# Upward stage of a feed-forward block: pinned squares, later use of mixed blocks, evacuation in parts

## The chip, the cores and the metric

The kernel runs on one core of one Trainium2 chip. Its time is the device time of one launch in microseconds (us), the median of several runs. The core has five engines with a queue each, which run their instructions in order: PE (TensorE, matmul), DVE (VectorE), ACT (ScalarE), POOL (GpSimd) and SP (SyncE), which here issues nearly all DMAs. PEld is PE's loading of weights.

## The reference

One block of a diffusion transformer on 2048 tokens of width 1024. A mixer comes first (gated linear attention and retention, both directions), then a convolutional feed-forward part, then a norm. The change concerns the weights of both, and above all the upward half of the feed-forward part:

```python
def _conv_ffn(h, w_up_l, conv_w_l, conv_b_l, w_down_l):
    gate, up = jnp.split(h @ w_up_l, 2, axis=-1)
    L = gate.shape[1]
    pad = CONV_W // 2
    gp = jnp.pad(gate, ((0, 0), (pad, pad), (0, 0)))
    gate = sum(gp[:, j:j + L] * conv_w_l[j] for j in range(CONV_W)) + conv_b_l
    return (jax.nn.silu(gate) * up) @ w_down_l
```

D_FF is 2816, CONV_W 3, and all inputs are float32.

## The kernel before

**Products.** Every big product is made of half-precision pairs (a high part and the rest), three matmuls for one (`mm3`, lines 84 to 86), and of 2x2 blocks with seven block products instead of eight (a Strassen-like scheme, Winograd's form). The left factor needs seven mixed blocks: four raw ones a11, a12, a21, a22 and three sums of them; two of the products, 0 and 1, use raw blocks alone. `left_blocks` yields them step by step; `emit` makes the high part on ACT and the rest on DVE, `add` makes the sums on POOL, in place.

**The upward stage** (`ffn_up`) goes over 11 pairs of column blocks j (columns j and j + 11 of 22). For each j it runs four *units*: `ty` 0 (gate) and 1 (up), each for the token halves t 0 and 1. A unit is seven passes of 12 matmuls of 128x512, which `unit` takes in the order 0, 1, 5, 6, 4, 3, 2; after passes 1, 4, 3 and 2 `evac` takes a result away. For the gate (`gate_evac`) this is the convolution: a centre tap on ACT, the two side taps on DVE, the edges to the neighbouring blocks, and a Silu when a half is whole. For up (`up_evac`) it is a product with the gate.

**Background work.** Between the passes `work(n)` draws n steps from a list of generators, `self.bg`, first come first served:

- `up_weights(j, ty)` loads two raw tiles `wur` (SP), squares them on ACT (line 1474, the sum of squares by row comes with it), sums the squares over rows by 16 matmuls with a column of ones (`col`, line 1476) and over everything by two more (`allsum`, line 107), derives a scale on DVE, and makes the seven blocks `w7`.
- `down_blocks(j)` loads two rows of the down weights, `wdb`, squares them on ACT (line 1513), forms four differences in place on POOL (line 1516), and stores them to `wdd`.
- `act_pairs(j, t, act)` makes the seven mixed blocks of the activations as pairs `st` and stores them to `actd` (seven stores for each half).

`wur` and `wdb` share the tag "wr", which has two buffers. So the up half's blocks must be done before the down rows can be loaded, and the down rows' differences must be stored before the gate weights of j + 1 can be loaded.

**Order.** The program's order is a priority only. A scheduler with a timing model sets the order of instructions on each engine when the kernel is built, and waits are put in after that; so code that moves in one place can turn the order elsewhere. `keep_in_program_order`, used by the change, holds an instruction in the program's order on its engine.

Of the kernel before, what the change touches and what calls it, by code (L numbers as in the profile page):

```python
# [18 lines left out]
P = 128  # L19
SEQ = 2048  # L20
D = 1024
# [21 lines left out]
RING = 10  # L43
SEQUENCE = 0, 1, 5, 6, 4, 3, 2
# [6 lines left out]
class Kern:  # L51
# [427 lines left out]
    def left_blocks(self, a, emit, add):  # L479

        a11, a12, a21, a22 = a
        emit(0, a11)
        yield
        emit(1, a12)
        yield
        emit(3, a22)
        add(a22, a21, a22, ALU.add)  # L487
        yield
        emit(4, a22)
        add(a21, a11, a21, ALU.subtract)  # L490
        yield
        emit(6, a21)
        add(a11, a22, a11, ALU.subtract)
        yield
        emit(5, a11)
        add(a12, a12, a11, ALU.subtract)
        yield
        emit(2, a12)
        yield
# [136 lines left out]
    def pair_blocks(self, raws, W, s, neg):  # L636

        nc = self.nc

        def emit(m, v):  # L640
            sc = neg if m == 3 else s
            nc.scalar.activation(W[m][:, 0], v, AF.Copy, scale=sc)  # L642
            nc.vector.scalar_tensor_tensor(W[m][:, 1], v, sc, W[m][:, 0], ALU.mult, ALU.subtract)  # L643
        blocks = [r[:, 4 * c:4 * c + 4] for r in raws for c in range(2)]
        yield from self.left_blocks(blocks, emit, nc.gpsimd.tensor_tensor)

    def scales(self, ssq, dqx, tag, bank="tu"):

        nc, kp = self.nc, self.kp
        s, i = self.pow2(self.wp, self.allsum(ssq, bank), 1, "w")  # L650
# [9 lines left out]
    def head_weights(self, h):  # L660
# [11 lines left out]
        for nm, tag, cols in want:  # L672
# [7 lines left out]
            def start(nm=nm, tag=tag, raws=raws, st=st):  # L680
# [7 lines left out]
                s, neg, dq = self.scales(ssq, self.dqx[:, 0:1] if h else None, "dq" + nm)  # L688
# [10 lines left out]
            def more(st=st):  # L699
                next(st["steps"], None)  # L700
                next(st["steps"], None)
# [757 lines left out]
    def up_weights(self, j, ty):  # L1459
# [10 lines left out]
        ssq = kp.tile([P, 2], F32, tag="ssqw2", bufs=2, name="ssqw")  # L1470
        col = self.ps("sc", [P, 2], "col")
        for i in range(2):
            sq = W[5 + i].rearrange("p a k n -> p (a k n)").bitcast(BF16)
            nc.scalar.activation(sq, raw[i].rearrange("p k n -> p (k n)"), AF.Square, scale=4.0, accum_out=ssq[:, i:i + 1])
            for k in range(KT):
                nc.tensor.matmul(col[:, i:i + 1], sq[:, k * P:(k + 1) * P], self.onesb, start=k == 0 and i == 0,
                                 stop=k == KT - 1 and i == 1, skip_group_check=True)
        yield
        s, neg, dq = self.scales(ssq, self.dqx[:, 1:2], ("dqz", "dqvg")[ty], "sc")
# [23 lines left out]
    def down_blocks(self, j):  # L1503
# [7 lines left out]
        for i, r in enumerate(rows):  # L1511
            junk = self.slot_tile([P, D], F16, "vg", "st")
            nc.scalar.activation(junk, r, AF.Square, scale=self.ias[:, j:j + 1], accum_out=self.wq[:, 2 * j + i:2 * j + i + 1])
# [22 lines left out]
    def gate_evac(self, j, t, act, ends):  # L1536

        nc = self.nc
        tap = self.W[j, 0][1]
        stt = nc.vector.scalar_tensor_tensor  # L1540

        def evac(f, half, c, s):
# [6 lines left out]
            nc.scalar.activation(a[:, o:o + G], c, AF.Identity, bias=self.cw[:, fi:fi + 1], scale=tp(1))  # L1549
# [3 lines left out]
            nc.scalar.copy(edge[:, n], view(c, 0, [[G - 1, 2]]))  # L1553
            stt(a[:, o + 1:o + G], c[:, :G - 1], tp(0), a[:, o + 1:o + G], ALU.mult, ALU.add)
            stt(a[:, o:o + G - 1], c[:, 1:], tp(2), a[:, o:o + G - 1], ALU.mult, ALU.add)
            ends[f][n] = True
            col = lambda x, i: act[x // 2][f][:, x % 2 * G + i:x % 2 * G + i + 1]
            for x in (n - 1, n):
                if x in ends[f] and x + 1 in ends[f] and x < 3:
                    stt(col(x, G - 1), edge[:, x + 1, 0:1], tp(2), col(x, G - 1), ALU.mult, ALU.add)  # L1560
                    stt(col(x + 1, 0), edge[:, x, 1:2], tp(0), col(x + 1, 0), ALU.mult, ALU.add)
            if n == 2:
                nc.scalar.activation(act[0][f], act[0][f], AF.Silu)
            if t and 2 in ends[f] and 3 in ends[f]:
                nc.scalar.activation(a, a, AF.Silu)
# [11 lines left out]
    def act_pairs(self, j, t, act):  # L1577
# [4 lines left out]
        def emit(m, v):  # L1582
            p = self.slot_tile([P, 2, G], F16, "vg", "st")
            nc.scalar.activation(p[:, 0], v, AF.Copy, scale=s)  # L1584
            nc.vector.scalar_tensor_tensor(p[:, 1], v, s, p[:, 0], ALU.mult, ALU.subtract)  # L1585
            nc.sync.dma_start(self.actd[m][t][:, j], p)
        blocks = [act[f][:, c * G:c * G + G] for c in range(2) for f in range(2)]
        yield from self.left_blocks(blocks, emit, nc.gpsimd.tensor_tensor)

    def ffn_up(self):  # L1590
        for j in range(NJ):
            self.bg.append(self.up_weights(j, 1))
            act = [[self.slot_tile([P, 2 * G], F32, KEPT[2 * ((2 * j + t) % 3) + f], "act") for f in range(2)] for t in range(2)]
            ends = [{}, {}]
            for ty in range(2):
                for t in range(2):
                    evac = self.gate_evac(j, t, act, ends) if ty == 0 else self.up_evac(j, t, act)
                    for _ in self.ffn_unit(self.W[j, ty][0], self.feats[t], evac, t):
                        self.work(2)
                    if ty == 0 and t == 0:  # L1600
                        self.bg.append(self.down_blocks(j))
                    if ty == 1:
# [214 lines left out]
```

## Time and profile before

| what | value |
| --- | --- |
| runs of the kernel | 2800.43 us median of 3 (2798.17 to 2802.12) |
| the profiled execution | 2800.01 us, span 2797.2 us |
| granted clock of PE, mean | 0.962 |
| mixer and output product | 0 to 1503.84 us |
| upward stage | 1503.84 to 2386.52 us |
| downward stage | 2386.52 to 2797.2 us |

The span goes from the first instruction to the last; the run's time holds a little more around it. In the profile's rows, `L84 PE MATMUL pa<-feat,w` is a matmul issued by line 84 that writes a PSUM tile named pa and reads the tiles feat and w. A wait row names the engine that waited, then whom it waited for.

### The profile page before, as it was taken

To read this page: it belongs to the slowest core of one execution; us is meant where nothing else is said; L and a number is where in the kernel's file an instruction comes from. 1 tells how busy PE (TensorE), PEld (TensorE's weight loads), DVE (VectorE), ACT (ScalarE), POOL (GpSimd) and SP (SyncE) were. 2 spreads that over 40 slices of the span, in tenths; PEclk is the share of its full clock that TensorE was granted. 3 is DMA by queue.
4 is the path that set the end of the run, shared out by engine and by line. 5 is a ranking of instruction groups with operands and counts; after the bars stand their busy time and mean duration, and the time that the engine had idled before them with its cause. 6 is when DMAs were issued, how large, how long until landed. Compare 5 with 4: busy or idle time off the path is not lost.

```text
span 2797.2 us, 56207 instructions
## 1 busy us (share of the span) xinstructions
PE 2575.3 (92%) x22829; PEld 1696.0 (61%) x22829; DVE 1820.0 (65%) x3568; ACT 1335.1 (48%) x2858; POOL 773.9 (28%) x905
## 2 busy tenths in 40 slices
PE   5789998999988988898999999999999999999998
PEld 2678887888888877887444444444444444444443
DVE  4998676776666565456465777677777777532553
ACT  5776456564543433345445555555555554411211
POOL 3642121121222222112334443334333333000111
PEclk7899999999999999998999999999999999999999
DMA  8224332342447675656621322232233323743652
GB/s 289 99 92 145 126 122 92 130 145 88 137 167 235 195 247 178 218 185 185 207 91 46 98 95 93 104 109 95 95 105 102 106 94 138 263 183 141 224 188 102
DMA packets 213523, 402.35 MB, mean 144 GB/s; under 512 B 16271, under 2 KB 98419, under 8 KB 208656
## 3 DMA queue, kind: packets, MB, share of 16 engines
q1 hardware_dynamic: 209856, 390.20, 41.1%
q10 hardware_dynamic: 3104, 8.40, 1.1%
q8 instruction: 178, 2.92, 0.4%
q14 instruction: 81, 0.66, 0.1%
q0 software_dynamic: 304, 0.17, 0.0%
HBM read 298.57 MB, written 91.75 MB: 140 GB/s over the span
## 4 chain that ended last, share of the span: by engine, by line
PE 54%; DVE 21%; DMA 9%; ACT 6%; issue 6%; POOL 4%; ACTq 0%; SPq 0%; DVEq 0%; POOLq 0%
PE pa L84 5%; PE pa L85 5%; PE pa L86 5%; PE pd L85 5%; PE pd L84 5%; PE pd L86 5%; PE pc L84 2%; PE pc L85 2%; PE pc L86 2%; DVE w L643 2%; DMA wur<-in_w_up_dram 2%; PE opp L86 2%; PE opp L85 2%; PE opp L84 2%; DMA wdb<-in_w_down_dram 2%
## 5 line engine op out<-in xcount | busy, mean ns | idle before, releaser
L84 PE MATMUL pa<-feat,w 128*128 128x512 f16 x704 | 267.0, 384 | 10.9 <-ACT ta L543 10.3
L85 PE MATMUL pa<-feat,w 128*128 128x512 f16 x704 | 270.4, 384 | 0.0
L86 PE MATMUL pa<-feat,w 128*128 128x512 f16 x704 | 268.9, 385 | 0.0
L85 PE MATMUL pd<-wd,actl 128*128 128x512 f16 x616 | 233.3, 379 | 0.0
L86 PE MATMUL pd<-wd,actl 128*128 128x512 f16 x616 | 233.3, 379 | 0.0
L84 PE MATMUL pd<-wd,actl 128*128 128x512 f16 x616 | 232.6, 379 | 0.6 <-ACT wd L1627 0.6
L85 PEld LDWEIGHTS <-w 128*128 128x128 f16 x1232 | 121.5, 99 | 157.4 <-issue 21.3
L86 PEld LDWEIGHTS <-w 128*128 128x128 f16 x1232 | 121.5, 99 | 148.6 <-issue 5.8
L84 PEld LDWEIGHTS <-w 128*128 128x128 f16 x1232 | 123.2, 100 | 143.2 <-issue 5.7
L85 PEld LDWEIGHTS <-hx 128*128 128x128 f16 x1824 | 185.9, 102 | 15.9 <-issue 13.4
L84 PEld LDWEIGHTS <-hx 128*128 128x128 f16 x1824 | 186.1, 102 | 2.3
L86 PEld LDWEIGHTS <-hx 128*128 128x128 f16 x1824 | 185.4, 102 | 3.1 <-issue 1.9
L1585 DVE SCALAR_TENSOR_TENSOR st<-act,modT,st 128x512 f16<-128x512 f32 x154 | 146.3, 975 | 55.8 <-ACT st L1584 55.8
L84 PE MATMUL pa<-w_vg,hx 128*128 128x128 f16 x800 | 151.3, 227 | 7.5 <-ACT ct L543 3.9
L85 PE MATMUL pa<-w_vg,hx 128*128 128x128 f16 x800 | 151.1, 227 | 0.0
L86 PE MATMUL pa<-w_vg,hx 128*128 128x128 f16 x800 | 151.1, 227 | 0.0
L1584 ACT ACTIVATE st<-act,modT 128x512 f16<-128x512 f32 x154 | 107.5, 718 | 79.8 <-POOL act L487 19.6
L84 PE MATMUL pc<-feat,w 128*128 128x512 f16 x352 | 135.1, 384 | 2.8 <-ACT tb L543 1.5
L643 DVE SCALAR_TENSOR_TENSOR w<-wur,p2s,w 128x512 f16<-128x512 f32 x132 | 111.1, 859 | 37.2 <-ACT w L642 37.2
L85 PE MATMUL pc<-feat,w 128*128 128x512 f16 x352 | 134.6, 382 | 0.0
L86 PE MATMUL pc<-feat,w 128*128 128x512 f16 x352 | 134.1, 382 | 0.0
L85 PEld LDWEIGHTS <-w_z 128*128 128x128 f16 x1072 | 108.0, 101 | 37.4 <-issue 25.7
(549 smaller groups left out, 7565.3 us busy)
## 6 DMA issues: line engine op xcount, KB each, us to landing
hx<-hxd SPq DMA_DIRECT2D x212, 512.0 KB, 4.8
actd<-st SPq DMA_DIRECT2D x154, 256.0 KB, 2.0
actl<-actd SPq DMA_DIRECT2D x28, 1024.0 KB, 5.1
wur<-in_w_up_dram SPq DMA_DIRECT2D x44, 512.0 KB, 4.0
raw<-in_w_in_dram SPq DMA_DIRECT2D x36, 512.0 KB, 4.5
wm<-in_w_mod_dram SPq DMA_DIRECT2D x64, 256.0 KB, 4.8
hxd<-hx SPq DMA_DIRECT2D x28, 512.0 KB, 3.4
wdb<-in_w_down_dram SPq DMA_DIRECT2D x22, 512.0 KB, 3.6
```

Of the source, the lines that this page charges most:

```text
L84: mm(ps, lhs(0), rhs(0), start=start, stop=False, skip_group_check=True)
L85: mm(ps, lhs(0), rhs(1), start=False, stop=False, skip_group_check=True)
L86: mm(ps, lhs(1), rhs(0), start=False, stop=stop, skip_group_check=True)
L643: nc.vector.scalar_tensor_tensor(W[m][:, 1], v, sc, W[m][:, 0], ALU.mult, ALU.subtract)
L1584: nc.scalar.activation(p[:, 0], v, AF.Copy, scale=s)
L1585: nc.vector.scalar_tensor_tensor(p[:, 1], v, s, p[:, 0], ALU.mult, ALU.subtract)
```

## The change

1. `left_blocks` has separate calls for the high part (`hi`) and the rest (`lo`), a step apart. Block 3 comes first, the three POOL sums follow in the next steps, and the blocks that use them come behind: 3, 0, 1, 4, 6, 5, 2. It yields nine steps instead of seven; the mixer's weights, which use it too, take three steps at a time instead of two.
2. In `up_weights` the two squares are a step each, pinned in the program's order on ACT; an empty step follows; the sums on PE come after it, and the scale a step later. The down rows' squares are pinned too.
3. `gate_evac` no longer issues its parts at once: centre, sides and Silu go into `self.parts`, and `follow` issues one part of each after each pass.
4. `ffn_up` hands out the loads ahead (`ahead`, with idle steps), starts both halves of j + 1 while j runs, waits for what is needed (`until`), and draws 1.7 or 2.3 steps a pass for gate and up, instead of 2.

```diff
-    def left_blocks(self, a, emit, add):
+    def left_blocks(self, a, hi, lo, add):
...
+        hi(3, a22)
+        yield
+        lo(3, a22)
+        hi(0, a11)
         add(a22, a21, a22, ALU.add)
         yield
-        emit(4, a22)
+        lo(0, a11)
+        hi(1, a12)
         add(a21, a11, a21, ALU.subtract)
...
+        for i in range(2):
+            self.tc.keep_in_program_order(nc.scalar.activation(sqs[i], raw[i].rearrange("p k n -> p (k n)"), AF.Square, scale=4.0,
+                                                               accum_out=ssq[:, i:i + 1]))
+            yield
+        yield
         col = self.ps("sc", [P, 2], "col")
...
-        yield
-        s, neg, dq = self.scales(ssq, self.dqx[:, 1:2], ("dqz", "dqvg")[ty], "sc")
+        total = self.allsum(ssq, "sc")
+        yield
+        s, neg, dq = self.scales(total, self.dqx[:, 1:2], ("dqz", "dqvg")[ty])
...
+            self.parts.append([centre, sides, silu])
...
+    def ahead(self, steps, idle=0):
+        next(steps)
+        yield
+        for _ in range(idle):
+            yield
+    def follow(self):
+        for p in self.parts:
+            p.pop(0)()
+        self.parts = [p for p in self.parts if p]
+    def until(self, steps):
+        while steps in self.bg:
+            self.work(1)
...
+    def ffn_pair(self, j, U):
+        act = []
+        ends = [{}, {}]
+        D = self.down_blocks(j)
+        self.bg += [U[j, 1], self.ahead(D, 3)]
+        for ty in range(2):
+            self.until(U.pop((j, ty), None))
+            for t in range(2):
...
+                for _ in self.ffn_unit(self.W[j, ty][0], self.feats[t], evac, t):
+                    self.due += RATE[ty] if j else 2
+                    self.work(int(self.due))
+                    self.due -= int(self.due)
+                    self.follow()
+                if ty == 1:
+                    U[j, "act", t] = self.act_pairs(j, t, act[t])
+                    self.bg.append(U[j, "act", t])
+            if ty == 0:
+                self.bg.append(D)
+                if j + 1 < NJ:
+                    for i, idle in ((0, 4), (1, 0)):
+                        U[j + 1, i] = self.up_weights(j + 1, i)
+                        self.bg.append(self.ahead(U[j + 1, i], idle))
+                        if i == 0:
+                            self.bg.append(U[j + 1, 0])
```

What the scheduler makes of it, at three places of the pair j = 5. First ACT, from the down rows' squares (`st<-wdb`) to the squares of the next gate weights (`w7<-wur`). Before:

```order
L1513 ACTIVATE st_25668,modT_162<-wdb_25651,modT_162 128x1024
L1563 ACTIVATE act_25382<-act_25382 128x1024
L1513 ACTIVATE st_25670,modT_162<-wdb_25653,modT_162 128x1024
L543 COPY ta_25606<-pa_25608 128x512
L543 COPY ta_25753<-pa_25755 128x512
L1549 ACTIVATE act_25385<-ta_25606,cw_161,taps_25159 128x512
L1553 COPY edge_25498<-ta_25606 128x2
L1474 ACTIVATE w7_25778,ssqw_25780<-wur_25769 128x1024
```

After, from the centre tap of the gate's last pass (line 1576) on:

```order
L1576 ACTIVATE act_25533<-pa_25538,cw_161,taps_25227 128x512
L1577 COPY edge_25416<-pa_25538 128x2
L1594 ACTIVATE act_25534<-act_25534 128x1024
L1533 ACTIVATE st_25771,modT_162<-wdb_25730,modT_162 128x1024
L1533 ACTIVATE st_25773,modT_162<-wdb_25732,modT_162 128x1024
L554 COPY ta_25734<-pa_25736 128x512
L1594 ACTIVATE act_25533<-act_25533 128x1024
L554 COPY tb_25735<-pc_25801 128x512
L1488 ACTIVATE w7_25834,ssqw_25836<-wur_25797 128x1024
```

The down squares moved from the middle of the gate's second unit to behind its last pass (`pa_25538`), and the weights' squares from among that unit's evacuation to behind the first copies of the unit after it (`pa_25736`, `pc_25801`).

Second PE, where the first sums of those squares stand. Before, `pa_25755` is the first up unit, in its pass 5:

```order
L84 MATMUL pa_25755<-feat_20720,w7_25507 128x512
L85 LDWEIGHTS w7_25507
L85 MATMUL pa_25755<-feat_20720,w7_25507 128x512
L86 LDWEIGHTS w7_25507
L86 MATMUL pa_25755<-feat_20720,w7_25507 128x512
L1476 LDWEIGHTS w7_25778
L1476 MATMUL col_25781<-onesb_21514,w7_25778 128x1
```

After, `pb_25927` is the second up unit, in its pass 1:

```order
L85 MATMUL pb_25927<-feat_21595,w7_25553 128x512
L86 LDWEIGHTS w7_25553
L86 MATMUL pb_25927<-feat_21595,w7_25553 128x512
L1495 LDWEIGHTS w7_25834
L1495 MATMUL col_25866<-onesb_21514,w7_25834 128x1
```

The sums moved by most of a unit. Counted in these orders, PE has 126 matmuls of passes between the up total (`allsum`) and these sums before, 147 after; and from their own total to the first use of the new gate blocks 102 before, 30 after. For the up half's blocks that is 72 before and 33 after. In the mixer's stage PE's order changes too, in some 240 places from the first projection on, with the same instructions.

Third SP, where the raw up weights of j + 1 are loaded. Before, behind one store of activation pairs:

```order
L1466 DMA wur_25771<-in_w_up_dram 128x8x128
L1586 DMA actd00_93<-st_25938 128x1024
L1466 DMA wur_26151<-in_w_up_dram 128x8x128
L1466 DMA wur_26153<-in_w_up_dram 128x8x128
L1586 DMA actd10_95<-st_25942 128x1024
```

After, between the last store of the first half and the first of the second half:

```order
L1621 DMA actd20_97<-st_26071 128x1024
L1480 DMA wur_25980<-in_w_up_dram 128x8x128
L1480 DMA wur_25982<-in_w_up_dram 128x8x128
L1621 DMA actd31_100<-st_26090 128x1024
L1621 DMA actd01_94<-st_26109 128x1024
```

The load moved behind six more stores, and its squares (not shown) to behind the first copy of the next gate's second unit.

115 lines of the change are left out of this document (61 added, 54 removed).

## The prediction

> **What bounds the kernel now.** I read the page, then the share of each engine by stage, then in the upward stage PE's waits, and last one column pair in order of time.
>
> ```profile
> span 2797.2 us, 56207 instructions
> PE 2575.3 (92%) x22829; PEld 1696.0 (61%) x22829; DVE 1820.0 (65%) x3568; ACT 1335.1 (48%) x2858; POOL 773.9 (28%) x905
> ...
> 0.00:1503.84 1503.84, 1335.33 (x16813) 1128.08 (x16814) 989.41 (x2164) 775.56 (x1894) 413.24 (x561) 0.94 0.48 158
> 1503.84:2386.52 882.68, 838.97 (x4153) 385.10 (x4152) 658.08 (x1155) 479.10 (x810) 325.82 (x229) 0.98 0.31 103
> ...
> 1503.84:1597.04 93.20, 83.36 (x409) 39.18 (x408) 73.31 (x122) 55.49 (x96) 37.90 (x32) 0.93 0.21 65
> 1597.04:1679.05 82.01, 76.79 (x378) 34.95 (x376) 60.47 (x107) 46.31 (x78) 31.91 (x22) 0.98 0.33 111
> 1679.05:2311.95 632.90, 604.31 (x3010) 277.06 (x3009) 468.80 (x827) 341.83 (x576) 232.97 (x160) 0.99 0.30 101
> 2311.95:2386.52 74.57, 74.51 (x361) 33.92 (x360) 55.50 (x102) 35.46 (x60) 23.04 (x16) 1.00 0.46 160
> ...
> 1979.03:1997.16 18.13, 18.13 (x86) 1.00 0.44 147
> 1997.16:2016.13 18.97, 18.97 (x105) 1.00 0.26 97
> 1730.60:1733.90 3.30, 3.30 (x10) 0.51 0.21 79
> 1809.10:1812.50 3.40, 3.40 (x9) 0.51 0.21 77
> 1887.60:1891.00 3.40, 3.40 (x10) 0.51 0.24 84
> 2123.20:2126.60 3.40, 3.40 (x11) 0.50 0.21 77
> 1891.20:1894.60 3.40, 3.40 (x18) 1.00 0.00 0
> ```
>
> The columns of the window rows are length, then busy time (count) of PE, PEld, DVE, ACT, POOL, then granted clock; the rows from 1979.03 on are PE alone. The upward stage is 882.68 us long (j = 0, j = 1, j = 2 to 9, j = 10 are the four rows under it). One undisturbed unit, 84 matmuls, is 18.13 us, 0.2158 us a matmul; a unit with one group of column sums is 18.97, so a group costs 0.84. A column pair j of four units and two groups would then take 4 x 18.13 + 2 x 0.84 = 74.2 us. Eight of them took 632.90, 79.1 each: 39.3 us are lost there. j = 1 loses 7.8, j = 10 with one group 1.2, j = 0 19.0, part of it the second norm's transposes. At a granted clock near 0.5 a stretch of 3.4 us holds some 10 matmuls instead of 18: 8 x 0.2158 = 1.7 us lost. The four such rows are all there are in j = 2 to 9, each just after a pair of waits.
>
> ```profile
> PE col L1476 <- ACT w L1474: 24.5, 16, 2.0
> PE pa L84 <- ACT ta L543: 4.1, 5, 1.8
> ...
> L1474 ACT ACTIVATE w<-wur 128x1024 bf16<-128x1024 f32 x32 | 33.8, 1057 | 73.4 <-DMA wur<-in_w_up_dram 73.4
> ...
> wur<-in_w_up_dram SPq DMA_DIRECT2D x44, 512.0 KB, 4.0
> ...
> PE pa L84 <- ACT ta L543: 4.7, 1, 4.7
> PE col L1476 <- ACT w L1474: 2.6, 2, 1.9
> ```
>
> The first three rows are j = 2 to 9 (two of PE's waits, then ScalarE's squares and what they wait for), the fourth is the page's row of the raw up-projection loads (4.0 us from issue to landing), the last two are j = 0. So 39.3 = 24.5 (column sums wait for squares) + 4.1 (a bank's copy) + 4 x 1.7 = 6.8 (half clock) + 3.9 spread. And the squares are late because the raw weights land late. One pair in order of time:
>
> ```profile
> 1932.47 0.58 PE L107 MATMUL allsum<-ssqw,ones 128*128 128x1 f32 x4
> 1946.61 2.35 SPq L1509 DMA_DIRECT2D wdb<-in_w_down_dram  x2
> 1950.34 1.15 ACT L1513 ACTIVATE st<-wdb,modT 128x1024 f16<-128x1024 f32 x1 [1.66 <-issue]
> 1951.66 5.39 POOL L1516 TENSOR_TENSOR wdb<-wdb 128x512 f32<-128x512 f32 x4 [5.67 <-ACT st L1513]
> 1956.52 0.38 SPq L1466 DMA_DIRECT2D wur<-in_w_up_dram  x1
> 1960.93 1.06 ACT L1474 ACTIVATE w<-wur 128x1024 bf16<-128x1024 f32 x1 [4.60 <-DMA wur<-in_w_up_dram]
> 1961.63 0.38 SPq L1466 DMA_DIRECT2D wur<-in_w_up_dram  x1
> 1965.51 1.06 ACT L1474 ACTIVATE w<-wur 128x1024 bf16<-128x1024 f32 x1 [1.69 <-DMA wur<-in_w_up_dram]
> 1962.14 0.35 PE L1476 MATMUL col<-onesb,w 128*128 128x1 bf16 x8 [1.43 <-ACT w L1474]
> 1966.72 0.35 PE L1476 MATMUL col<-onesb,w 128*128 128x1 bf16 x8 [1.61 <-ACT w L1474]
> 1966.93 0.58 PE L107 MATMUL allsum<-ssqw,ones 128*128 128x1 f32 x4
> ```
>
> From one total (the up half's) to the next gate half's squares runs one chain through the two "wr" buffers: up blocks, down rows, their squares, four differences on POOL, their stores, then the raw gate weights. The second square ends at 1966.57, 34.1 us after the total. PE reached the first sums at 1960.71 and the second at 1965.11, and waited 1.43 and 1.61.
>
> **The change, part by part.** No matmul, activation, POOL sum or DMA is added or removed in number; everything is a move.
>
> (1) Where the sums stand. In the orders PE has 126 matmuls between the up total and the next gate sums before, 147 after, and 12 more to the second group. So PE gets there 0.4 + 147 x 0.2158 = 32.1 us after the total, and at 35.0 for the second group.
>
> (2) The chain. The down squares, now pinned, stand on ScalarE behind the centre and one Silu of the gate unit's last pass, which ends 71 matmuls (15.3 us) after the total.
>
> ```profile
> 1967.29 1.04 ACT L1565 ACTIVATE act<-act 128x1024 f32<-128x1024 f32 x1
> 1968.23 0.76 ACT L1549 ACTIVATE act<-pa,cw,taps 128x512 f32<-128x512 f32 x1
> 1970.84 0.15 DVE L99 TENSOR_SCALAR p2s<-p2i 128x1 int32<-128x1 int32 x1
> 1971.98 1.32 ACT L642 ACTIVATE w<-wur,p2s 128x512 f16<-128x512 f32 x2
> 1972.72 1.42 DVE L643 SCALAR_TENSOR_TENSOR w<-wur,p2s,w 128x512 f16<-128x512 f32 x2 [1.40 <-ACT w L642]
> ...
> L643 DVE SCALAR_TENSOR_TENSOR w<-wur,p2s,w x122: 736/744/1437, 1559.5 to 2340.7; 128x512 f16<-128x512 f32 x122
> L487 POOL TENSOR_TENSOR wur<-wur x20: 1263/1712/1773, 1587.8 to 2332.1; 128x512 f32<-128x512 f32 x20
> ```
>
> Centre 0.76 and Silu 1.04 with its wait for VectorE make 2.3, so they start at 0.4 + 15.3 + 2.3 = 18.0; before, on landing, at 17.9. The tail from there to the second square's end was 1966.57 - 1950.34 = 16.2, and its DMAs and POOL differences keep their order on SP and POOL: 34.2 against 35.0. The first square ends at 18.0 + 11.7 = 29.7 against 32.1. Slack 0.8 and 2.4 us. VectorE late with the taps' sides eats the 0.8; I bound the remaining wait per pair by 0 and 2.0 (the longest wait before) and take 0.3, near zero because the slack is positive: 8 x 0.3 = 2.4. Gain 24.5 - 2.4 = 22.1. Pinning also puts PSUM copies behind the squares; they find their weights landed, so they wait for nothing. If the load is late, the copy of the next unit's first pass, and PE on its bank, queue behind it.
>
> (3) Half clock. With no pair of waits over 1.3 us the four halvings go: 6.8, bounds 0 and 6.8. The Trainium skill (TensorE: Matmul & The Clock Gate, "HAM oscillation — how this bites in real kernels") wants an idle gap of over some 3.4 us before the clock halves; by that rule waits of at most 2.0 do not do it, the halvings have another cause, and the sum is 6.8 longer (rival D). The trace speaks against the rule: the clock halves within microseconds of a pair of waits, with no idle stretch of that length.
>
> (4) The up half's load now stands on SP behind the first half's seven stores of activation pairs and ahead of the second's seven, and its squares a unit later, behind the next gate unit's first copy: they find their data landed. The 16 column waits of j = 2 to 9 are two in each, all of the gate half, so there is nothing to gain here; the cover of the load, 4.0 us, is that unit of 18.
>
> (5) Blocks used sooner after their sums. Gate block 0 was needed 102 matmuls after its total, now 30; up block 0 72, now 33. The scale is ready 1970.84 - 1966.93 = 3.9 us after the total and 3, 0 now come first: two high parts of 0.66 end at 5.2, two low parts of 0.71 at about 6.1. PE wants the high part at 0.4 + 30 x 0.2158 = 6.9 and the low at 7.8. Slack 1.7. Later blocks have 3 us or more. Bounds per place 0 and 3; I take 0.15: 16 x 0.15 = 2.4 lost. Mixed blocks three steps behind their sums give ScalarE no POOL waits; they were off the path.
>
> (6) Evacuation in parts holds the last pass's bank up to two steps (5 us) longer. The next use of it is a unit, 18 us, away: nothing, and if that cover went, the bank wait (4.1) would grow. Of 4.1 + 3.9 I take 5.0 as gained, since copies no longer stand behind squares that wait for DMA; bounds 0 and 8.
>
> j = 2 to 9: 22.1 + 6.8 + 5.0 - 2.4 = 31.5. j = 1: the same causes, 5.5 of 7.8. j = 10: 0.5 of 1.2. j = 0: its 4.7 is a copy behind the second norm's casts, which stay, and the up half's sums move later, so the chain behind them starts later; I take 0, bounds -8 and +8. Sum 37.5.
>
> (7) Head stage. left_blocks serves it too, and the scheduler turned much of its order around. Its blocks are made a tick ahead of use, so I see no price; PE idles 1503.84 - 1335.33 = 168.5 us there, and as an estimate 6% of that, 10 us, either way.
>
> 2800.0 (the profiled execution, 2797.2 span and 2.8 around it) - 37.5 = 2762.5. The median of the runs, 2800.43, is 0.4 above: 2763.
>
> **The rivals.** A, the chain stays late: if the down squares start 2 us later (VectorE, 468.80 of 632.90 busy, must finish the sides first), the second sums wait 1.2 more, and half the halvings stay: 8 x 1.2 + 3.4 + 5.0 of (6) not gained = 18 less, about 2781; with more lateness up to 2795. For it: slack is only 0.8. Against: it starts on ScalarE, not on a landing.
>
> B, slower: the blocks come too late at (5). One low part takes 1.437 instead of 0.744 when POOL works; if the four VectorE operations of the way in and a backlog cost 1.0 each, block 0 is 4.0 - 1.7 = 2.3 late, and a halving of 1.7 can follow. Over 20 places that is 20 x 4.0 = 80: 2843. It decides against the change from 37.5 / 20 = 1.9 us a place. The Trainium skill (SBUF — State Buffer, "SBUF: two separate sides") says a VectorE operation with two SBUF inputs and a GpSimd one lock each other out; the trace agrees, 0.744 to 1.437 and on POOL 1.263 to 1.773. Against it: that happened before as well, and PE shows no wait for a low part.
>
> C, everything lost comes back: 39.3 + 7.8 + 1.2 and 8 of j = 0, 56: 2744, less with a lucky head stage. D, the halvings stay though the waits go: 6.8 more, 2770; against it, each of the four rows follows a pair of waits. E, the change does nothing, since the chain's length, not the place of the sums, is the period: the same total to total, 2798. Against: PE's place moves 4.5 us, more than the 3.0 waited.
>
> **How the numbers follow.** Forecast, 2747 to 2778: 0.61. A: 0.14. C: 0.11. D: 0.05. E: 0.03. B: 0.06. The range leaves out B, E, the far end of A and a bit of C: 2742 to 2785. A measurement tells 0.2%, 5.6 us, from no change. Faster: forecast, C, D, nearly all of A, 0.90; same 0.03, E; slower 0.07, B and a costly head stage.
>
> **What would show it.** The column row among PE's waits falls from 24.5 to a few us; a pair takes 75 to 76 us; the granted clock of j = 2 to 9 is 1.00; the squares' row loses its 73.4 of waiting for the up half. A new row of PE waiting for w (VectorE or ScalarE) is B; the head stage off 1503.84 by over 10 us is (7).

## The result and the profile after

The changed kernel took 2827.6 us (median of 4, 2822.43 to 2830.52), the kernel before 2800.8 beside it: 1.0095 of it, 95% interval 1.0077 to 1.0112. It is slower by 27 us where 37 less were forecast. The profiled execution took 2822.43 us, its span is 2820.7; it is the fastest of the four, so some 4 of the 27 us stand in no row below.

The stages of the changed kernel; columns as in the prediction's window rows (length, then busy time and count of PE, PEld, DVE, ACT, POOL, then granted clock, the DMA engines' share and GB/s). The first three rows are the mixer, the upward and the downward stage, the others j = 0, j = 1 and j = 2 to 9:

```profile
0.00:1503.36 1503.36, 1328.49 (x16813) 1121.57 (x16814) 994.42 (x2164) 776.48 (x1895) 413.89 (x562) 0.95 0.48 158
1503.36:2405.62 902.26, 843.40 (x4153) 385.86 (x4152) 679.19 (x1151) 470.68 (x809) 332.73 (x228) 0.98 0.30 100
2405.62:2820.70 415.08, 402.47 (x1864) 183.61 (x1863) 172.13 (x255) 81.23 (x156) 34.80 (x116) 0.99 0.49 181
1503.36:1602.98 99.62, 83.53 (x410) 38.82 (x409) 73.56 (x120) 54.84 (x95) 37.73 (x31) 0.93 0.18 59
1602.98:1686.32 83.34, 77.53 (x378) 34.91 (x377) 62.23 (x105) 43.45 (x74) 30.94 (x22) 0.96 0.30 101
1686.32:2330.00 643.68, 607.66 (x3010) 278.23 (x3008) 484.71 (x824) 335.88 (x577) 240.16 (x161) 0.99 0.29 98
```

The mixer stage is unchanged (-0.5) in these two executions. Of the 23.5 us by which the span grew, j = 2 to 9 hold 10.8 (632.90 to 643.68), j = 0 holds 6.4, j = 1 1.3, j = 10 1.0, the downward stage 4.4. PE's waits in j = 2 to 9, and the one of the downward stage:

```profile
PE col L1495 <- ACT w L1488: 24.8, 16, 3.5
PE pa L85 <- ACT ta L554: 5.5, 7, 1.0
PE pa L87 <- DVE w L657: 4.1, 3, 1.4
PE pa L85 <- DVE tb L588: 1.5, 7, 0.3
...
PE pd L85 <- ACT wd L1699: 3.5, 1, 3.5
```

The sums of the weights' squares wait as long as before (24.5), though they stand elsewhere. The bank waits, in which PE waits until a PSUM tile has been copied away, grew (4.1 to 7.0, for `ta` and `tb`), a wait for the low part of a block is new (4.1), and the excess of matmuls at half clock, worked out from their spacing, rose from 6.7 to 8.1 us: 8.7 of the 10.8 us. One pair in order of time (parts of SP, ACT, PE and DVE, from the up total):

```profile
1951.23 0.58 PE L108 MATMUL allsum<-ssqw,ones 128*128 128x1 f32 x4
1964.23 3.97 SPq L1529 DMA_DIRECT2D wdb<-in_w_down_dram  x2
1968.47 0.81 ACT L1576 ACTIVATE act<-ta,cw,taps 128x512 f32<-128x512 f32 x1 [2.41 <-DVE ta L588]
1970.23 1.06 ACT L1591 ACTIVATE act<-act 128x1024 f32<-128x1024 f32 x1 [0.87 <-DVE act L1586]
1971.20 0.76 ACT L1576 ACTIVATE act<-pa,cw,taps 128x512 f32<-128x512 f32 x1
1971.90 1.06 ACT L1594 ACTIVATE act<-act 128x1024 f32<-128x1024 f32 x1
1972.86 1.14 ACT L1533 ACTIVATE st<-wdb,modT 128x1024 f16<-128x1024 f32 x1
1973.99 1.14 ACT L1533 ACTIVATE st<-wdb,modT 128x1024 f16<-128x1024 f32 x1
1984.34 1.06 ACT L1488 ACTIVATE w<-wur 128x1024 bf16<-128x1024 f32 x1 [6.74 <-DMA wur<-in_w_up_dram]
1988.94 1.06 ACT L1488 ACTIVATE w<-wur 128x1024 bf16<-128x1024 f32 x1 [2.23 <-DMA wur<-in_w_up_dram]
1985.54 0.25 PE L1495 MATMUL col<-onesb,w 128*128 128x1 bf16 x4 [1.07 <-ACT w L1488]
1990.14 0.35 PE L1495 MATMUL col<-onesb,w 128*128 128x1 bf16 x8 [1.66 <-ACT w L1488]
1990.36 0.58 PE L108 MATMUL allsum<-ssqw,ones 128*128 128x1 f32 x4
1995.92 1.36 DVE L657 SCALAR_TENSOR_TENSOR w<-wur,neg,w 128x512 f16<-128x512 f32 x1
1997.87 3.43 DVE L657 SCALAR_TENSOR_TENSOR w<-wur,p2s,w 128x512 f16<-128x512 f32 x2
1999.68 0.39 PE L87 MATMUL pa<-feat,w 128*128 128x512 f16 x1 [1.38 <-DVE w L657]
```

The first down square (`st<-wdb`) starts 21.6 us after the total, with no wait marked: its row had landed 5.1 us earlier, and it stands pinned behind two centres and two Silus, of which the first ones wait for VectorE. The second weight square ends 38.8 us after the total. PE reaches the sums about where the prediction said (33.2 us after the total for 32.1), and waits.

### The profile page after: what moved, and what is told of

It is laid out like the page before. It is cut to its first block, busy times and chain, and to the rows that moved or that the text cites. A ratio compares the mean times of both kernels' runs of the same rounds, so it can differ in the third digit from the quotient of the medians.

```text
span 2820.7 us, 56389 instructions
## 1 busy us (share of the span) xinstructions
PE 2574.4 (91%) x22829; PEld 1691.0 (60%) x22829; DVE 1845.7 (65%) x3568; ACT 1328.4 (47%) x2858; POOL 781.4 (28%) x905
## 3 DMA queue, kind: packets, MB, share of 16 engines
q1 hardware_dynamic: 209856, 390.20, 40.8%
## 4 chain that ended last, share of the span: by engine, by line
PE 26%; DVE 12%; issue 10%; DMA 7%; POOL 5%; ACT 3%; ACTq 0%; POOLq 0%; SPq 0%; DVEq 0%
PE pd L85 5%; PE pd L87 5%; PE pd L86 5%; DVE w L657 3%; DVE st L1620 3%; DMA wdd<-wdb 2%; PE opp L87 2%; PE opp L85 2%; PE opp L86 2%; DMA wur<-in_w_up_dram 2%; DVE act L1580 1%; DMA Q<-K 1%; DVE act L1604 1%; DMA wdb<-in_w_down_dram 1%; PE pa L85 1%
## 5 line engine op out<-in xcount | busy, mean ns | idle before, releaser
L85 PE MATMUL pa<-feat,w 128*128 128x512 f16 x704 | 267.3, 384 | 15.8 <-ACT ta L554 11.4
L1620 DVE SCALAR_TENSOR_TENSOR st<-act,modT,st 128x512 f16<-128x512 f32 x154 | 161.9, 1063 | 107.5 <-ACT st L1616 107.5
L86 PEld LDWEIGHTS <-hx 128*128 128x128 f16 x1824 | 183.6, 101 | 18.4 <-issue 15.9
L87 PEld LDWEIGHTS <-hx 128*128 128x128 f16 x1824 | 183.1, 100 | 3.8 <-issue 2.4
L85 PEld LDWEIGHTS <-hx 128*128 128x128 f16 x1824 | 184.0, 101 | 2.0
L85 PE MATMUL pa<-w_vg,hx 128*128 128x128 f16 x800 | 149.2, 225 | 11.4 <-DVE cb L588 7.5
L86 PE MATMUL pa<-w_vg,hx 128*128 128x128 f16 x800 | 148.9, 225 | 0.1
L87 PE MATMUL pa<-w_vg,hx 128*128 128x128 f16 x800 | 148.6, 225 | 0.0
L657 DVE SCALAR_TENSOR_TENSOR w<-wur,p2s,w 128x512 f16<-128x512 f32 x132 | 142.6, 1102 | 2.9 <-ACT w L654 2.9
L85 PE MATMUL pa<-hx,w_z 128*128 128x256 f16 x464 | 128.7, 277 | 10.8 <-DVE V L596 4.1
L87 PE MATMUL pc<-feat,w 128*128 128x512 f16 x352 | 133.7, 380 | 1.4 <-DVE w L657 1.4
L86 PE MATMUL pc<-feat,w 128*128 128x512 f16 x352 | 133.6, 380 | 1.3 <-POOL feat L1378 1.3
```

The source lines that it names most:

```text
L85: mm(ps, lhs(0), rhs(0), start=start, stop=False, skip_group_check=True)
L86: mm(ps, lhs(0), rhs(1), start=False, stop=False, skip_group_check=True)
L87: mm(ps, lhs(1), rhs(0), start=False, stop=stop, skip_group_check=True)
L657: nc.vector.scalar_tensor_tensor(W[m][:, 1], v, sc(m), W[m][:, 0], ALU.mult, ALU.subtract)
```

## The experiments

Each kernel was timed against the kernel before on the same chip; the ratios are to that. The stage times and waits (us) are of one profiled execution each. "Chain" is the mean over j = 2 to 9, worked out from the trace, from the last matmul of the up total to the start of the first down square and to the end of the second weight square; it was 17.6 / 34.0 before, 21.4 / 38.8 after.

**Undoing one part of the change.** `d_free`: the down squares lose their pin.

```diff
-            self.tc.keep_in_program_order(nc.scalar.activation(junk, r, AF.Square, ...))
+            nc.scalar.activation(junk, r, AF.Square, ...)
```

> The changed kernel with the down rows' squares no longer pinned; all else stays. In ScalarE's order they stand two copies and one centre tap earlier, ahead of the Silus, and the gate sums stand 139 matmuls after the up total instead of 147. Theory 1 (the squares' pinned place starts the chain late: in the changed kernel they begin 21.5 us after the up total, 5 us behind the landing of their first row): the first begins about 16.5 after the total, the second at 20.9 instead of 22.7, the second weight square ends about 34.5 instead of 38.8 after the total, PE wants it at 33.5; the column waits of j = 2 to 9 fall from 24.8 to about 6 us and one to three of the five halvings go: 2802 to 2810. Theory 2 (the blocks used sooner after their sums and the copies set the time, the squares' place is harmless): 2825 to 2830, column waits over 20 us.

`evac_once`: the evacuation's parts at once.

```diff
-            self.parts.append([centre, sides, silu])
+            centre()
+            sides()
+            silu()
```

> The changed kernel with the gate's centre, sides and Silu issued at once after a pass, as before; both pins stay. With the parts issued earlier in the program, the pinned down squares come back to the place in ScalarE's order that they have without their pin. Theory 1: the same as without the pin, 2802 to 2810, within 4 us of that run, since pin and parts delay the squares only together. Theory 2 (evacuation in parts is a gain by itself, since copies no longer stand behind it): copies come later, PE's waits for ta grow from 5.5 to 8 us or more, and the time is 2828 to 2836.

`w_free`: the same edit as d_free, on the weights' squares (`sqs[i]`) instead.

> The changed kernel with the weights' squares no longer pinned, the down rows' squares still pinned. The order around the down squares is the changed kernel's. Theory 1: nothing changes, 2823 to 2831, column waits 23 to 26 us. Rival (the pinned weight squares hold the copies behind them and the loss is theirs): column and bank waits fall by 15 us, 2808 to 2814.

`old_blocks`: `left_blocks` in the old order.

```diff
-        hi(3, a22)
-        yield
-        lo(3, a22)
-        hi(0, a11)
-        add(a22, a21, a22, ALU.add)
+        emit(0, a11)
+        yield
+        emit(1, a12)
+        yield
+        emit(3, a22)
+        add(a22, a21, a22, ALU.add)
...
```

> The changed kernel with the blocks made in the old order (0, 1, 3, 4, 6, 5, 2, high and low part in one step, the sums two steps ahead of their use as before). In PE's order the gate sums come in two groups 151 and 167 matmuls after the up total (147 and 159 in the changed kernel), and the new blocks are used 22 matmuls after the total. Theory 1 (start of the chain): the down squares still stand behind the Silus, so the chain is as late, but PE comes 1.7 us later to the second group: column waits 24.8 to about 12 us, 2812 to 2820. Theory 2 (sooner use of the blocks): the 4.1 us of waits for a low part of w change, to 0 if the new order makes them, or to 10 or more since the place is 8 matmuls nearer: 2823 or 2835.

| run | ratio (95%) | j = 2 to 9 | column waits | chain |
| --- | --- | --- | --- | --- |
| changed kernel | 1.0095 (1.0077 to 1.0112) | 643.7 | 24.8 | 21.4 / 38.8 |
| d_free | 1.0077 (1.0052 to 1.0102) | 629.4 | 19.1 | 15.8 / 33.2 |
| evac_once | 1.0049 (1.0031 to 1.0066) | 628.5 | 19.1 | 15.8 / 33.3 |
| w_free | 1.0164 (1.0137 to 1.0191) | 658.0 | 25.6 | 21.6 / 38.6 |
| old_blocks | 1.0030 (1.0014 to 1.0045) | 638.7 | 9.8 | 21.4 / 38.3 |

Two different edits put the down squares back and give the same: the chain 5.5 us shorter, a stage 14 to 15 us shorter. So pin and parts together made the chain late. But the column waits fell by 6 us only, where 19 were expected: the sums now stand earlier as well (139 matmuls after the total instead of 147). The other 8 us are the waits for low parts, which go, and for banks. PE's waits in j = 2 to 9 of d_free:

```profile
PE col L1495 <- ACT w L1488: 19.1, 8, 3.0
PE pa L85 <- ACT ta L554: 2.9, 7, 0.7
```

Over the whole kernel the gain of evac_once is clear (1.0049 against 1.0095); that of d_free is not, its interval overlaps that of the changed kernel (its runs went from 2804 to 2825, the profiled one was the lowest). w_free was a miss: without the pin the up half's squares turned the order of the copies, and PE waited 15.5 us for the bank copy `tb`, which stood behind activation pairs that wait for POOL. In old_blocks the chain is as late as in the changed kernel, but the sums stand 151 and 167 matmuls after the total, so PE waits 9.8 for columns; it waits 21 for scale and low parts, 22 matmuls being too few.

**Parts alone, in the kernel before.** `b_late6`: six empty steps between the next gate half's squares and their sums.

```diff
+        if ty == 0 and j:
+            for _ in range(6):
+                yield
         col = self.ps("sc", [P, 2], "col")
```

> The kernel before with one change: six empty steps between the squares of the next gate half's raw weights and their sums on PE. In PE's order the sums move from 126 and 138 matmuls after the up total to 156 (both groups), their total to 168; the new blocks are then used 72 matmuls after it instead of 102. Theory 3 (a scheduler puts the sums where its own model expects the squares, some 3 us before they are really there, whatever the chain does, so the waits go only if the sums are put later than that by hand): PE comes at 0.4 + 156 x 0.2158 = 34.1 us after the up total, where the second square ends; column waits of j = 2 to 9 fall from 24.5 to under 3 us, the four halvings (6.8) and most of the spread go with them, j = 1 gains some 4: 0.986 to 0.990 of the kernel before. Theory E (the chain is the period, PE waits for it wherever the sums stand): 0.998 to 1.002, the waits at another place.

`b_blocks`: point 1 of the change alone (`left_blocks` and its callers). `b_parts`: point 3 alone:

```diff
+            self.parts.append([centre, sides, silu])
...
                         self.work(2)
+                        self.follow()
```

> The kernel before with the new left_blocks alone (high and low part a step apart, blocks 3, 0, 1, 4, 6, 5, 2, nine steps). The scheduler puts the gate sums 121 and 134 matmuls after the up total instead of 126 and 138, about 1 us sooner. Theory 3: nothing in the chain gets faster, so PE waits about 1 us a pair longer, column waits 24.5 to about 32 us, the rest within the head stage's 10 us: 1.000 to 1.006. Theory 2 (the sooner use is the loss): new waits for a low part of w of 10 us or more. Step 5 of the prediction, 0.15 us a place: no visible wait for w.

> The kernel before with the gate's evacuation in parts alone (centre, sides and Silu a pass apart). Sums and down squares stand where they stood: 126 and 138 matmuls after the up total. Theory 3: the chain is the same, column waits 23 to 26 us, and 0.998 to 1.002. Step 6 of the prediction: bank waits (4.1) and half the spread go, 5 us, 0.998. Rival: the last pass's bank is held up to 5 us longer and the sides on DVE come late, bank waits of 8 us or more: 1.002 to 1.005.

`a_early` is the changed kernel with the up half's steps ahead of the activation pairs (`k` is the place of the first of these in the list).

```diff
-        self.bg += [U[j, 1], self.ahead(D, 3)]
+        self.bg.insert(k, U[j, 1])
+        self.bg.append(self.ahead(D, 3))
```

> The changed kernel with one change: the steps of the up half's weights come ahead of the activation pairs of the pair before, no longer behind them. In PE's order the up total moves from 111 to 24 matmuls after a pair's start, the next gate sums from 258 and 270 to 243, so 219 matmuls (47 us) lie between instead of 147. Theory 3: the chain (38.8 us in the changed kernel, the squares still pinned behind the Silus) is covered; the column waits for the gate half go from 24.8 to under 3 us and the five halvings with them, and the up sums, whose raw weights land only just before, wait up to 0.5 us a pair: 0.997 to 1.003 of the kernel before (the changed kernel 1.0095). Theory 2 (sooner use of the blocks, evacuation in parts): no less than 1.006. Rival within theory 3: the up sums now wait 1 to 2 us a pair, and the halvings stay: 1.003 to 1.007.

> The changed kernel with one change: the steps of the up half's weights come ahead of the activation pairs of the pair before, no longer behind them. In PE's order the up total moves from 111 to 24 matmuls after a pair's start, the next gate sums from 258 and 270 to 243, so 219 matmuls (47 us) lie between instead of 147. Theory 3: the chain (38.8 us in the changed kernel, the squares still pinned behind the Silus) is covered; the column waits for the gate half go from 24.8 to under 3 us and the five halvings with them, and the up sums, whose raw weights land only just before, wait up to 0.5 us a pair: 0.997 to 1.003 of the kernel before (the changed kernel 1.0095). Theory 2 (sooner use of the blocks, evacuation in parts): no less than 1.006. Rival within theory 3: the up sums now wait 1 to 2 us a pair, and the halvings stay: 1.003 to 1.007.

| run | ratio (95%) | j = 2 to 9 | column waits | chain |
| --- | --- | --- | --- | --- |
| b_late6 | 0.9986 (0.9974 to 0.9997) | 625.6 | 6.0 | 17.9 / 34.7 |
| b_blocks | 1.0171 (1.0155 to 1.0186) | 656.8 | 15.3 | 19.1 / 35.2 |
| b_parts | 0.9959 (0.9946 to 0.9972) | 618.7 | 16.1 | 16.5 / 32.4 |
| a_early | 1.0098 (1.0083 to 1.0114) | 641.8 | 23.4 | 33.1 / 49.0 |

The surprise is b_blocks. PE's waits in its j = 2 to 9:

```profile
PE col L1489 <- ACT w L1487: 15.3, 8, 2.1
PE pc L84 <- ACT tb L553: 13.3, 8, 1.8
PE pa L84 <- DVE tb L587: 9.7, 7, 1.4
PE pa L84 <- DVE act L1568: 3.8, 5, 1.1
```

No wait for w among them; PE waits for banks. One place in order of time (POOL, DVE, ACT, PE; the up total was at 1947.42):

```profile
1954.49 1.71 POOL L487 TENSOR_TENSOR wur<-wur 128x512 f32<-128x512 f32 x1 [6.35 <-DVE w L656]
1954.32 2.42 DVE L656 SCALAR_TENSOR_TENSOR w<-wur,p2s,w 128x512 f16<-128x512 f32 x2
1958.35 1.22 DVE L1574 SCALAR_TENSOR_TENSOR act<-edge,taps,act 128x1 f32<-128x1 f32 x1
1964.85 0.68 DVE L587 TENSOR_TENSOR ta<-pb,ta 128x512 f32<-128x512 f32 x1
1965.57 0.81 ACT L1562 ACTIVATE act<-ta,cw,taps 128x512 f32<-128x512 f32 x1 [3.46 <-DVE ta L587]
1968.32 0.57 ACT L553 COPY tb<-pc 128x512 f32<-128x512 f32 x1
1968.93 0.38 PE L84 MATMUL pc<-feat,w 128*128 128x512 f16 x1 [1.78 <-ACT tb L553]
```

POOL's first sum begins among the low parts of the raw blocks: two of them take 2.42 us, where two took 1.42 in the row of the prediction. VectorE falls behind, reaches the evacuation's add `ta<-pb` 17.4 us after the total (14.1 in the kernel before; 1.5 of these 3.3 us it brings along, its scale being ready at 4.4 instead of 2.9), ScalarE waits for it 3.46 us with the centre, and the bank copy behind the centre is late.

In b_late6 the column waits fell to 6.0 (under 3 were expected), but bank waits took their place (4.1 to 15.5, for `ta`), and the whole gain is 0.1% where 1.0 to 1.4% were expected: the squares stayed where they stood on ScalarE, wait there for their load, and copies queue behind them. In a_early, expected at 0.997 to 1.003, the column waits moved whole: the gate half's sums wait 2 us in all, the up half's 21, up to 3.8 each, since their raw weights land too late for the earlier place.

**What in the new blocks costs.** `b_order`: the new order, high and low part in one step (`emit(3)`, then `emit(0)` with the first sum, `emit(1)` with the second, and so on). `b_split`: the old order, the two a step apart (`hi(0)`; `lo(0)`, `hi(1)`; `lo(1)`, `hi(3)`; ...). `bl_dve`: all of the new `left_blocks`, with the weights' sums on VectorE:

```diff
-        yield from self.left_blocks(blocks, hi, lo, nc.gpsimd.tensor_tensor)
+        yield from self.left_blocks(blocks, hi, lo, nc.vector.tensor_tensor)
```

> The kernel before with the new order of blocks alone: 3, 0, 1, 4, 6, 5, 2, the four sums on POOL one step ahead of where they stood, high and low part in one step, seven steps as before. (With hi and lo split as well it took 1.0171 of the kernel before.) Theory 4 (the order is the loss: POOL's sums now begin while the low parts of the raw blocks run, an operation of VectorE beside POOL takes 0.7 to 1.0 us longer, VectorE reaches the evacuation's combining add some 3 us later, and ScalarE, in order, keeps the bank copies waiting behind the centre tap): 1.012 to 1.018, sums of waits for ta, tb and act of 20 us or more in j = 2 to 9, as with the whole new left_blocks (27). Theory 5 (the loss comes from the steps: nine instead of seven, so everything behind in the list starts later): 0.998 to 1.004.

> The kernel before with only the split of high and low part into steps of their own (eight steps instead of seven), the old order 0, 1, 3, 4, 6, 5, 2 and the sums' old places. Theory 4 (order): 0.998 to 1.004. Theory 5 (steps): 1.012 to 1.018, the downward stage's first wait for wd over 3 us.

> The kernel before with the new left_blocks, but the up weights' four sums on VectorE instead of POOL (an add of this size takes 0.68 us there, 1.6 on POOL). Theory 4 (collision of VectorE and POOL): the low parts of w fall from 0.98 to 0.75 us, the edge columns that met POOL from 1.2 to 0.21, the four added sums cost 2.7 us of VectorE a set, and the blocks end some 3 us sooner: most of the 1.7% comes back, 0.995 to 1.003. If the new order costs by itself (blocks too late for PE, steps): 1.010 to 1.018.

b_order took 1.0184 (1.0168 to 1.0200), b_split 0.9999 (0.9990 to 1.0008), bl_dve 0.9925 (0.9907 to 0.9943); j = 2 to 9 took 656.4, 631.1 and 613.9 (656.8 in b_blocks). So the order is the loss, not the steps, and without POOL's sums beside it it is none. The group rows of the low parts of w in j = 2 to 9 (busy time, mean ns), of the kernel before, b_blocks and bl_dve:

```profile
L643 DVE SCALAR_TENSOR_TENSOR w<-wur,p2s,w 128x512 f16<-128x512 f32 x96 | 78.5, 837 | 28.5 <-ACT w L642 28.5
```

```profile
L656 DVE SCALAR_TENSOR_TENSOR w<-wur,p2s,w 128x512 f16<-128x512 f32 x96 | 91.9, 977 | 10.5 <-ACT w L653 10.5
```

```profile
L656 DVE SCALAR_TENSOR_TENSOR w<-wur,p2s,w 128x512 f16<-128x512 f32 x96 | 71.5, 749 | 0.0
```

bl_dve also shortens the mixer's stage, 1508.1 to 1485.0, and the chain's sums (0.68 us each instead of 1.6), and the scheduler put the column sums 145 matmuls after the up total instead of 121. So its gain is more than the collision alone, and the share of each is open.

**How the parts act together.** `a_rest` is old_blocks and evac_once in one, the rest of the change alone; `b_pb` is blocks and parts without the rest.

> The changed kernel without the new left_blocks and without the evacuation in parts: what is left of the change are the squares in steps of their own and pinned, the sums behind them, and the new hand-out of steps and loads. The up total stands 51 matmuls later in a pair than before (111 instead of 60), the gate sums 148 matmuls after it. Theory 6 (the rest is harmful by itself, since the late up total leaves the chain and the blocks only 189 matmuls, 40.8 us, to the next pair's first use, where the kernel before has 240): 1.004 to 1.010, with waits for low parts of w. Rival (the rest is a gain that the new blocks hide: with the new blocks it took 1.0049, they alone 1.0171): 0.985 to 0.995.

> The kernel before with the new left_blocks and the evacuation in parts, without the rest of the change. Theory 4, if both act on their own: 1.0171 - 0.0041 = 1.013 (1.010 to 1.016), bank waits of 20 us or more. Rival (parts take away what the blocks cost, since the evacuation no longer stands as a block behind the low parts): 0.998 to 1.006.

| | neither | blocks | parts | both |
| --- | --- | --- | --- | --- |
| without the rest | 1 | 1.0171 | 0.9959 | 1.0187 (1.0158 to 1.0215) |
| with the rest | 1.0068 (1.0045 to 1.0091) | 1.0049 | 1.0030 | 1.0095 |

The parts do not add up. Without the rest, where the up total is early, the new blocks cost 1.7%, and 2.3% beside the parts; with it they cost nothing clear alone (1.0049 against 1.0068) and 0.65% beside the parts. The parts gain 0.4% alone, and as much with the rest and the old blocks; beside the new blocks they gain nothing, and beside new blocks and pin they lose 0.5%. The rest costs 0.7% alone. Why the new blocks cost less where the up total is late is not shown.

`a_dve` is the changed kernel with the edit of bl_dve.

> The changed kernel with one change: the weights' four sums on VectorE instead of POOL, in the mixer's weights too. The order puts the gate sums 153 and 165 matmuls after the up total instead of 147 and 159. Theory 4 (collision): low parts of w 1.09 to 0.75 us, the blocks end 3 to 4 us sooner, so the chain does; column waits 24.8 to under 8 us, most halvings go, and the head stage gains some 20 us as it did in the kernel before (1508 to 1485): 0.986 to 0.996. Theory 1 (the pinned down squares behind the Silus alone are late, the sums do not matter): the stage stays, only the head gains: 1.001 to 1.005.

It took 1.0003 (0.9991 to 1.0014). The mixer's stage gained 18 us; j = 2 to 9 stayed (643.4). The expectation was half wrong, and its waits tell most:

```profile
PE pa L85 <- ACT w L654: 15.4, 8, 2.4
PE pa L87 <- DVE w L657: 11.7, 8, 1.6
PE col L1495 <- ACT w L1488: 0.2, 1, 0.2
```

With the chain 3.2 us shorter the column waits are gone, and PE waits as long for the first blocks instead, 27 matmuls behind their total. In the changed kernel 189 matmuls (40.8 us) lie between the up total and the next pair's first block; the chain (38.8) and, behind it, the scale and the first low part (7.3) need more. The wait of rival B, which had a chance of 0.06, is there as soon as the other is taken away.

**A better version.** `pl_1_2_2`: the kernel before with the evacuation in parts, the next gate half's squares pinned one and two steps later, their sums two steps behind (`far` is true for that half alone). `pl_dve`: the same with the weights' sums on VectorE.

```diff
+            for _ in range((1, 2)[i] * far):
+                yield
+            op = nc.scalar.activation(sqs[i], ...)
+            if far:
+                self.tc.keep_in_program_order(op)
+        for _ in range(2 * far):
+            yield
```

> A version put together from what the runs showed: the kernel before with the gate's evacuation in parts (alone 0.9959), and for the next gate half the squares of the raw weights pinned one and two steps later and their sums two steps behind them. In PE's order the two groups of sums stand 161 and 180 matmuls after the up total instead of 126 and 138, the new blocks are used 60 matmuls after the second. Theory 3 with the squares moved as well as the sums: with parts alone the second square ends 31.7 us after the total, PE comes at 34.7 and 38.9, so the column waits of j = 2 to 9 (16.1) and the halvings (4.9) go, and no copy stands behind a square that waits for its load: 0.984 to 0.989 of the kernel before. Theory E (waits only move, as with the sums alone put later, where the bank waits grew by 11 us): 0.994 to 0.998.

> The best version so far (evacuation in parts, squares and sums of the next gate half late; 0.9876) with the weights' four sums on VectorE instead of POOL. Pairs j = 2 to 9 stand at 595.6 of an ideal 593.6, so the upward stage has nothing to gain; theory 4 gives a gain of 15 to 20 us in the mixer's stage, where the same blocks are made: 0.979 to 0.984. Rival (the head stage's gain belonged to the new order of blocks, which is not in this version, or VectorE becomes the bound there): 0.986 to 0.990.

pl_1_2_2 took 0.9876 (0.9860 to 0.9893), pl_dve 0.9793 (0.9770 to 0.9817), 2.1% less than the kernel before. PE's only wait in j = 2 to 9 and that stretch, of pl_1_2_2; then the mixer's stage and the stretch of pl_dve:

```profile
PE pa L84 <- ACT ta L543: 0.6, 2, 0.4
...
1673.24:2268.85 595.61, 594.70 (x3010) 276.33 (x3008) 479.87 (x825) 337.48 (x577) 249.56 (x160) 1.00 0.32 107
```

```profile
0.00:1475.75 1475.75, 1321.35 (x16814) 1114.54 (x16815) 978.00 (x2228) 775.92 (x1897) 330.79 (x498) 0.95 0.49 161
...
1644.61:2239.90 595.29, 594.19 (x3009) 276.65 (x3008) 465.98 (x890) 340.29 (x573) 142.89 (x96) 1.00 0.32 107
```

A pair takes 74.4 us of the 74.2 that the prediction called ideal, at a granted clock of 1.00.

## Why the prediction was wrong

**What is lost was read rightly.** The 39.3 us of j = 2 to 9 are waits and half clock that follow from late squares; pl_1_2_2, with squares and sums put later than their data, got 37.3 of them back.

**(1) held.** PE stands 147 matmuls behind the up total and reached the sums at 33.2 us instead of 32.1, after a bank wait of 0.75.

**(2) failed, and carried the sum.** The down squares' start was put at 18.0 us by counting one centre and one Silu behind the last pass; two of each are still to run there, with VectorE's sides between, and the start is 21.4. The tail from there, put at 16.2, took 17.5. So the second square ends at 38.8 instead of 34.2, and the slack of 0.8 was a lack of 3.8. Of the 22.1 us of gain none came. d_free and evac_once show the start as the cause; they show also that the repair alone is worth 14 to 15 us of j = 2 to 9, since the order then calls for the sums earlier. The prediction treated a place that the scheduler chose as a free choice. It reads better as the scheduler's own forecast of when the squares are there: in five kernels PE came early (before, after, d_free, b_blocks, b_parts), and with the shorter chain of d_free and evac_once the place moved forward. That is inferred from the orders and not shown: with the sums on VectorE (bl_dve, a_dve) the chain is shorter and the place is later.

**(5) failed by its size.** 0.15 us a place, 2.4 in all, was taken; the bounds were 0 and 3. In the pair above PE gets block 0's low part 9.3 us after the gate total (1990.36), where 6.1 was put and 7.8 wanted: the low parts of block 3 and of the next two take 1.36 and 3.43 us, where 0.71 each was taken. So the slack of 1.7 was a lack of 1.5, and PE waits 1.38, in three of the eight pairs. Alone, the new order costs 23.9 us in j = 2 to 9, 1.5 a place, and there the price came another way, by VectorE's backlog, ScalarE's order and the banks. In the changed kernel the new blocks cost 18 us (old_blocks), 5 of them in j = 2 to 9; part stays hidden behind the column waits until these go (a_dve).

**(6) had the sign, not the size, and not in this company.** Alone, parts gained 14.2 us in j = 2 to 9 where 5.0 were taken, 8.4 of it in column waits, since the chain became 1.6 us shorter. Together with the pinned down squares the same parts put these behind the Silus, and evac_once is 15 us faster in the stage than the changed kernel.

**(3) and the small ones.** The halvings stayed because the waits did: 8.1 us at half clock instead of 6.7; without waits there are none (0.1 in pl_1_2_2), as the term said. j = 0 lost 6.4, inside its bounds of 8: its up total comes 15 us later. The downward stage's 4.4 was in no term: the first `wd` waits 3.5 us behind the last activation pairs, which b_blocks shows as well; b_split does not. (4) held: all 16 column waits are still of the gate half. (7) is not contradicted: the head moved by 0.5 in the profiled executions, but it varies by more than that from one execution to the next (below), so a price of a few us may hide there.

**The chances.** B was the rival on the other side, and the blocks were its matter; A, the late chain, was given 0.14 with 18 us less gain, as if only its slack could be lost. What happened is both, with (6) and (3) lost behind them.

## What to carry to other kernels

Read a scheduler's place for a waiting instruction as its forecast of the data, and compare that with the trace first. To take a wait away, move the whole group (here the squares on ScalarE and their sums on PE) later than the forecast, while there is room to the next use. Before code that makes something available sooner is taken as free, look at what runs beside it: low parts slowed by POOL's sums cost no wait where there is slack (they average 1.03 us in pl_1_2_2), while in b_blocks, at 0.98 us, an evacuation queues behind them and the kernel takes 1.7% more. Where one cycle holds two tight places, a shorter wait at one turns up at the other; only the room between them helps.

## What the hardware showed

An operation of VectorE on 128x1 elements took 1.22 us beside POOL's sum and ended with it (1942.85 and 1942.83), where it takes 0.21 free; one that reads PSUM (`pa`) beside the next sum took 0.74, its usual time (0.736 to 0.752 in all 22 of line 1554). Rows of the kernel before, DVE and POOL:

```profile
1941.63 1.22 DVE L1560 SCALAR_TENSOR_TENSOR act<-edge,taps,act 128x1 f32<-128x1 f32 x1
1942.77 0.74 DVE L1554 SCALAR_TENSOR_TENSOR act<-pa,taps,act 128x511 f32<-128x511 f32 x1
...
1941.10 1.73 POOL L490 TENSOR_TENSOR wur<-wur 128x512 f32<-128x512 f32 x1
1942.91 1.27 POOL L493 TENSOR_TENSOR wur<-wur 128x512 f32<-128x512 f32 x1
```

So it is a wait for the end of the other's operation, not a share of speed. The Trainium skill (SBUF — State Buffer, "SBUF: two separate sides") calls the shared ports an exclusive lock for operations with two SBUF inputs; these rows agree.

The clock halved after waits much shorter than the 3.4 us of the Trainium skill's rule in the prediction (TensorE: Matmul & The Clock Gate, "HAM oscillation — how this bites in real kernels"): a_dve's longest wait is 2.4 us, and matmuls at half clock cost it 18.9 us in j = 2 to 9; with no wait over 0.4 they cost 0.1 (pl_1_2_2). In a_dve the waits come in pairs, four matmuls apart, of 1.5 to 2.4 and 0.9 to 1.6 us. The trace decides against the rule as a threshold for one gap.

The mixer's stage varies with the same order of instructions. In the changed kernel, d_free, evac_once and a_early all engines run it in one and the same order, and it took 1502.3 to 1511.0 us. Over all kernels with sums on POOL it took 1496.6 to 1517.7: a mean of 1509.7 in the eight with block 3 first, 1503.4 in the seven others, so single executions say little of a few us there. With sums on VectorE it was 1475.8 to 1485.5 in three kernels, below all of these.
